# Two of the four rows of attention weights in each half of a head, turned by 32x32 blocks and DMAs through DRAM

## The chip, the cores and the metric

The kernel runs on one core of one Trainium2 chip. The metric is device time in microseconds (us) of one execution: 1113.87 us before the change, the median of three runs (1113.86 to 1114.06). The engines are named as in the profile: PE is TensorE (matmuls and transposes; PEld its weight loads), DVE is VectorE, ACT is ScalarE, POOL is GpSimd, and SP is the engine whose queue issues every DMA of this kernel. SBUF is the memory of 128 partitions beside the engines, PSUM the one that PE writes, DRAM the large one outside.

## What is computed

A trunk of two layers over 1024 positions of width 1024 in float32: a gated linear recurrence (RG-LRU), then an attention layer with a forget gate (FoX), each with a norm ahead and a residual, and a final norm. The change concerns the attention:

```python
def fox_mixer(h, w_in, b_f, w_out):          # 16 heads of 64
    q, k, v, gate, f_logit = ...              # slices of h @ w_in
    cum = cumsum(log_sigmoid(f_logit + b_f))
    def one_block(q_blk, cq_blk, start):      # 128 queries
        logits = einsum("bqhd,bkhd->bhqk", q_blk, k) / 8
        logits = logits + (cq_blk[..., :, None] - ck[:, :, None, :])
        logits = where(kpos <= qpos, logits, -1e30)
        p = softmax(logits)
        return einsum("bhqk,bkhd->bqhd", p, v)
    ...
    return (o * silu(gate)) @ w_out
```

## The kernel before

Almost every product is a sum of three: both factors are split into a high part that TensorE's float32r takes exactly and a low part (the rest), and high times high, high times low and low times high are added in PSUM. So each operand costs a rounding copy (to_hi, mostly ACT, L87) and a subtraction (to_lo, mostly DVE or POOL, L98). In the attention products the weights p are split and V comes with both parts side by side.

The recurrence layer fills the span up to about 405 us; its last projection, keys, queries, gates, values and the sums of the forget gate take it to about 510 us. From there to about 1086 us the 16 heads run one after the other, and the span ends with the last projection, the norm and the stores (tile "turn", L57 and L918 to L976).

A head has two halves c of 512 queries, and a half four rows i of 128 queries (i = 4c to 4c+3). Row i sees (i+1) blocks of 128 keys.

- maxima(hd, c) is a generator with one step a row: PE makes the logits S[queries, keys] (L57, tile S), DVE adds the mask and takes the row maximum (L731), ACT takes the exponential with its sum (L736) into p{i}, [128 queries, (i+1) x 128 keys]. Rows go in ascending order. A last step inverts the sums and sends them through DRAM (recd, recb), from where POOL scales the gate (L765).
- weigh(hd, c) needs p with the keys on the partitions. In steps of two key blocks it transposes every 128x128 block of p on PE against an identity (L61, tile pt in PSUM), ACT rounds the result into ph, DVE subtracts into pl, and PE adds V x ph and V x pl into O (L57). The products of a step are held until the step after it (held). A last step adds the halves of O (L810, L811).
- fill is a generator of other matmuls that don't depend on this head: keys, queries and gates of the next pair of heads, or for the last four heads the output projection. One unit is six matmuls of 512 columns.

The order on PE is written out by hand. In each of the strings below a digit is a step of that generator and a dot is a unit of fill; in the first, 0 is weigh(hd, 0) and 1 is maxima(hd, 1), in the second 0 is weigh(hd, 1) and 1 is maxima(hd + 1, 0). What is left of a generator is run at the end. Heads 12 to 15 have LAST, with more fill.

```python
ORDER = "1.0.1.1.1.0.0", "10.1.0.1.01.0.0"
LAST = "1..0.1..1..1.0.0", "10..1.0.1.01..0..0"
```

Each step on PE is put behind the one before with issue_after. The other engines' instructions are ordered by the scheduler of the tile framework and run in that order; where a tile is used again, the new writer waits for the old readers. S and pt share one tag of two PSUM buffers, ph and pl have three SBUF tiles each, and each p{i} has one.

All DMAs are issued by SP, in order. Weight tiles come through the tag "wf", four tiles (L108, L360, L533, L984), are split, and are used by PE. At the end of head hd, load(hd + 2) (L621 to L635) brings keys and queries of the head after the next into T and U, as soon as PE no longer reads them.

## Time and profile before

| | |
|---|---|
| timed, median of 3 | 1113.87 us |
| profiled execution, its own time | 1113.94 us |
| its span (first to last instruction) | 1112.2 us |
| granted clock of TensorE | 1.00 |
| DMA | 105.43 MB in 63558 packets, 31.1% of 16 engines' span |
| transposes of p on PE (L61) | 576 |
| splits of pt into ph and pl | 198 on ACT, 198 on DVE |

How to read the rows that follow in the prediction. A group has line, engine, operation, tiles "out<-in", shape and count, then busy us and mean ns of one, then the idle time of the engine just ahead of them and what ended it. A row of the timeline has start, length, engine, line, operation, tiles and count. A wait has who waited for whom, us in total, times and the longest. In a window stand its ends and length, then busy us (and instructions) of PE, PEld, DVE, ACT and POOL, the granted clock, the share of the DMA engines and GB/s. Matmuls overlap, so the mean of one is longer than the distance from one to the next.

### The profile page before, as it was taken

What the parts mean: (1) busy time and instruction counts of PE and PEld (TensorE: products, weight loads), DVE (VectorE), ACT (ScalarE), POOL (GpSimd) and SP (SyncE); (2) the same over time, 40 slices, a digit from 0 to 9 for tenths busy, and PEclk for the clock granted to TensorE, in tenths of its full rate; (3) what the DMA queues carried; (4) which work ended last, traced back from release to release, by engine and by line L of the source; (5) the groups of instructions that cost most, each with busy time, mean ns of one, the idle gap of its engine ahead of it and who ended that gap; (6) DMA issues with size and microseconds to landing.
All of it is one profiled execution on the core that took longest, in us unless ns stands there. A gap on an engine that the chain in (4) does not pass through costs nothing.

```text
span 1112.2 us, 15778 instructions
## 1 busy us (share of the span) xinstructions
PE 1101.9 (99%) x5697; PEld 935.1 (84%) x5697; DVE 755.0 (68%) x1266; ACT 582.4 (52%) x1075; POOL 166.1 (15%) x120
## 2 busy tenths in 40 slices
PE   9999999999999999999999999999999999999997
PEld 7787888888888888988888988889888898878886
DVE  8888755876669687756676566765667655576645
ACT  8487445355453665544555355544555544454435
POOL 1222212111111201421110100101002020010110
PEclk9999999999999999999999999999999999999999
DMA  6111111111112113443334224242142431655444
GB/s 239 48 57 43 51 54 43 48 53 42 62 35 75 48 54 129 129 112 118 101 90 103 91 69 109 72 113 96 53 122 75 103 108 38 185 159 185 142 147 189
DMA packets 63558, 105.43 MB, mean 95 GB/s; under 512 B 9364, under 2 KB 24340, under 8 KB 63480
## 3 DMA queue, kind: packets, MB, share of 16 engines
q1 hardware_dynamic: 63480, 104.42, 31.1%
q8 instruction: 45, 0.74, 0.3%
q14 instruction: 33, 0.27, 0.1%
HBM read 63.30 MB, written 15.93 MB: 71 GB/s over the span
## 4 chain that ended last, share of the span: by engine, by line
PE 93%; issue 3%; DVE 1%; ACT 1%; POOL 1%; DMA 1%; SPq 0%; DVEq 0%; POOLq 0%; ACTq 0%
PE gps L57 33%; PE ops L57 17%; PE ups L57 10%; PE vps L57 8%; PE S L57 6%; PE O L57 6%; PE pt L61 6%; PE turn L57 3%; PE gate L57 2%; POOL wl L98 1%; PE sscol L57 0%; DMA x<-in_xt 0%; DVE hl L232 0%; PE rsrow L57 0%; DMA wf<-in_w 0%
## 5 line engine op out<-in xcount | busy, mean ns | idle before, releaser
L57 PE MATMUL gps<-hh,wh 128*128 128x512 f32 x576 | 228.2, 396 | 0.0
L57 PE MATMUL gps<-hh,wl 128*128 128x512 f32 x576 | 225.6, 392 | 0.2 <-POOL wl L98 0.2
L57 PE MATMUL gps<-hl,wh 128*128 128x512 f32 x576 | 225.5, 392 | 0.0
L87 ACT CAST wh<-wf 128x512 fp32r<-128x512 f32 (+2 forms) x156 | 94.0, 607 | 141.8 <-PE gps L57 56.0
L736 ACT ACTIVATE p<-S,m 128x128 f32<-128x128 f32 (+7 forms) x128 | 94.9, 741 | 140.0 <-DVE m L731 139.1
L98 POOL TENSOR_TENSOR wl<-wf,wh 128x512 fp32r<-128x512 f32 (+1 forms) x60 | 95.6, 1600 | 382.2 <-ACT wh L87 321.7
L98 DVE TENSOR_TENSOR pl<-pt,ph 128x512 fp32r<-128x512 f32 (+1 forms) x198 | 98.7, 540 | 77.0 <-ACT ph L87 76.3
L57 PEld LDWEIGHTS gps<-hl,wh 128*128 128x128 f32 x576 | 108.2, 188 | 23.8
L57 PEld LDWEIGHTS gps<-hh,wl 128*128 128x128 f32 x576 | 108.5, 188 | 19.2 <-POOL wl L98 0.6
L57 PEld LDWEIGHTS gps<-hh,wh 128*128 128x128 f32 x576 | 108.5, 188 | 19.0
L731 DVE CUSTOM_DVE_ANT_0 S<-S,mask 128x128 f32<-128x128 f32 (+7 forms) x128 | 97.3, 760 | 34.2 <-PE S L57 29.6
L765 POOL TENSOR_TENSOR sg<-sg,recb 64x512 f32<-64x512 f32 x32 | 42.8, 1356 | 441.9 <-DMA recb<-recd 407.3
L87 ACT CAST ph<-pt 128x512 fp32r<-128x512 f32 (+1 forms) x198 | 83.5, 472 | 29.1 <-PE pt L61 23.9
L57 PE MATMUL S<-T,U 96*128 96x512 f32 (+7 forms) x384 | 91.7, 347 | 0.0
L98 DVE TENSOR_TENSOR wl<-wf,wh 128x512 fp32r<-128x512 f32 x96 | 68.3, 719 | 24.6 <-ACT wh L87 23.8
L375 DVE TENSOR_TENSOR x<-x,ops 128x512 f32<-128x512 f32 x80 | 54.1, 681 | 40.3 <-PE ops L57 40.3
L57 PEld LDWEIGHTS S<-T,U 128*128 128x128 f32 (+1 forms) x384 | 68.7, 189 | 12.5 <-ACT p L736 0.2
L61 PE MATMUL pt<-ident,p 128*128 128x128 f32 x576 | 79.2, 273 | 0.0
L61 PEld LDWEIGHTS pt<-ident,p 128*128 128x128 f32 x576 | 67.5, 140 | 11.5 <-issue 2.1
L57 PE MATMUL ups<-hh,wh 128*128 128x512 f32 x192 | 75.4, 394 | 1.0 <-ACT hh L89 0.4
L57 PE MATMUL ups<-hh,wl 128*128 128x512 f32 x192 | 75.0, 391 | 0.6 <-POOL wl L98 0.6
L57 PE MATMUL ups<-hl,wh 128*128 128x512 f32 x192 | 75.2, 391 | 0.2 <-DVE hl L232 0.2
(163 smaller groups left out, 2245.4 us busy)
## 6 DMA issues: line engine op xcount, KB each, us to landing
wf<-in_w SPq DMA_DIRECT2D x100, 256.0 KB
wf<-in_wo SPq DMA_DIRECT2D x64, 128.0 KB
U<-qkh SPq DMA_DIRECT2D x64, 128.0 KB
T<-qkh SPq DMA_DIRECT2D x28, 256.0 KB
x1d<-x SPq DMA_DIRECT2D x16, 256.0 KB
wf<-in_wv SPq DMA_DIRECT2D x16, 256.0 KB
U<-qkl SPq DMA_DIRECT2D x32, 128.0 KB
xp<-x1d SPq DMA_DIRECT2D x16, 256.0 KB
```

What stands on the lines that cost most here:

```text
L57: pe[0] = nc.tensor.matmul(*args, **kw)
L61: pe[0] = nc.tensor.transpose(*args)
L87: nc.scalar.copy(hi, src)
L98: return eng.tensor_tensor(lo, src, f32(hi), ALU.subtract)
L375: nc.vector.tensor_tensor(x, x, pt, ALU.add)
L731: masked[0] = nc.vector.tensor_tensor_reduce(S[:, :n], S[:, :n], mask[:, SEQ - n :], -1.0, -NEG, ALU.add, ALU.min, accum_out=m)
L736: seen[0] = nc.scalar.activation(p, S[:, :n], AF.Exp, bias=m, scale=-1.0, accum_out=sums[:, i : i + 1])
L765: nc.gpsimd.tensor_tensor(sg, sg, recs[hd // 2][rows, part], ALU.mult)
```

## The change

In every half but the lower half of head 0 (by_dma), the two longest rows of the four, i % 4 = 2 and 3, are turned without PE, except for the diagonal block of the longest (key block 4c+3), which PE still transposes.

- The two rows of a half lie in one tile (tag pp0 or pp1, two_rows): 2 x (4c+3) key blocks and the diagonal block behind them. This takes the place of p2, p3 and p6, p7.
- After the exponential of such a row, turn_row has DVE transpose its 4c+3 key blocks by 32x32 blocks into a tile "turn" (one buffer, 128 x 384 or 128 x 896), with an order of the columns in which each of the four quarters m of a key block is contiguous. A DMA on SP stores it into DRAM (turnd). After the second of the two rows, four more DMAs read it back, one for each m, into 32 partitions of the same tile from which the rows came, in runs of (4c+3) x 128 bytes.
- The rows go in descending order (reversed), in every half.
- weigh has near pieces, transposed by PE into PSUM as before, and far pieces, [128, 8, 32] views of the tile of two rows in SBUF (far_rows). Both are split into one ph and one pl, the near pieces first; the products are as they were. Where all rows of a key block are far, it has no near piece.
- To make room, wf has three tiles in place of four, fz, cp and res take other tags.

```diff
-        a = wpool.tile([P, room], F32, tag="wf", name="wf", bufs=4)[:, :n]
+        a = wpool.tile([P, room], F32, tag="wf", name="wf", bufs=3)[:, :n]
...
-        fz = const.tile([P, 8, HEADS], F32, name="fz")
+        fz = at.tile([P, 8, HEADS], F32, tag="yo", name="fz", bufs=2)
...
+        two_rows = {}
+        turnd = [dram.tile([P, 2, (4 * c + 3) * P], F32, name=f"turnd{c}") for c in range(2)]
+
+        def row_tile(i, n):
+            c, r = i // 4, i % 4 - 2
+            if r < 0:
+                return at.tile([P, n], F32, tag=f"p{i}", name="p", bufs=1)
+            size = (4 * c + 3) * P
+            if r:
+                two_rows[c] = at.tile([P, 2 * size + P], F32, tag=f"pp{c}", name="pp", bufs=1)
+            return two_rows[c][:, r * size : r * size + n]
+
+        def by_dma(hd, c):
+            return hd > 0 or c == 1
+
+        def turn_row(i, p):
+            c, r = i // 4, i % 4 - 2
+            nk = 4 * c + 3
+            t = at.tile([P, 7 * P], F32, tag="turn", name="turn", bufs=1)[:, : nk * P]
+            nc.vector.transpose(
+                t.rearrange("p (m k q) -> p k m q", m=4, q=32),
+                p[:, : nk * P].rearrange("p (k m q) -> p k m q", m=4, q=32),
+            )
+            nc.sync.dma_start(turnd[c][:, r], t)
+            if r == 0:
+                to = two_rows[c][:, : 2 * nk * P].rearrange("p (r b f) -> p r b f", r=2, b=4)
+                src = turnd[c].rearrange("(b p) r (m f) -> m p r b f", b=4, m=4)
+                for m in range(4):
+                    nc.sync.dma_start(to[32 * m : 32 * m + 32], src[m])
+
+        def far_rows(c):
+            return two_rows[c][:, : (8 * c + 6) * P].rearrange("p (b k q) -> p b k q", b=8, q=32)
...
-            for i in range(4 * c, 4 * c + 4):
+            for i in reversed(range(4 * c, 4 * c + 4)):
...
-                p = ps_[i] = at.tile([P, n], F32, tag=f"p{i}", name="p", bufs=1)
+                p = ps_[i] = row_tile(i, n)
...
+                if i % 4 > 1 and by_dma(hd, c):
+                    turn_row(i, p)
...
-                for jj in range(2):
-                    ks = slice((j0 + jj) * P, (j0 + jj + 1) * P)
-                    for q in range(qlo[jj], end, P):
-                        o = q - qlo[jj]
-                        transpose(A[:, jj, o : o + P], ps_[q // P][:, ks], ident)
...
+                near, far = [], []
+                for jj, j in enumerate((j0, j0 + 1)):
+                    rows = range(qlo[jj] // P, end // P)
+                    away = [i for i in rows if i % 4 > 1 and j < 4 * c + 3] if by_dma(hd, c) else []
+                    own = [i for i in rows if i not in away]
+                    for o, i in enumerate(own):
+                        transpose(A[:, jj, o * P : (o + 1) * P], ps_[i][:, j * P : (j + 1) * P], ident)
+                    w = len(own) * P
+                    near.append((A[:, jj, :w], slice(0, w)))
+                    far.append((j, slice(4 * (away[0] % 4) - 8, 8), slice(w, ns[jj])) if away else None)
...
+                for lo in range(2):
+                    for (ph, pl), (src, to) in zip(parts, near):
+                        if to.stop:
+                            split(src, ph[:, to], pl[:, to], lo)
+                for lo in range(2):
+                    for (ph, pl), f in zip(parts, far):
+                        if f:
+                            j, b, to = f
+                            split(far_rows(c)[:, b, j], *(z[:, to].rearrange("p (b q) -> p b q", q=32) for z in (ph, pl)), lo)
```

Here split(src, hi, low, lo) is to_hi on ACT for lo = 0 and to_lo on DVE for lo = 1.

More of the change, by code (lines that the diff above doesn't have):

```diff
@@ L267, in split_gates @@
         def split_gates(n):
-            wt = wpool.tile([P, 4, P], F32, tag="wf", name="wgf", bufs=4)[:, :2]
+            wt = wpool.tile([P, 4, P], F32, tag="wf", name="wgf", bufs=3)[:, :2]
             nc.sync.dma_start(wt, wg[n])
@@ L356, in out_weights @@
         def out_weights(g, d0, parts=wpool):
-            wt = wpool.tile([P, 4, P], F32, tag="wf", name="wf", bufs=4)
+            wt = wpool.tile([P, 4, P], F32, tag="wf", name="wf", bufs=3)
             for j in range(2):
@@ L531, in value_weights @@
                 if k < KT:
-                    wt = wpool.tile([P, 2, 256], F32, tag="wf", name="wf", bufs=4)
+                    wt = wpool.tile([P, 2, 256], F32, tag="wf", name="wf", bufs=3)
                     nc.sync.dma_start(wt, wv[g, :, k : k + 2])
@@ L658, in forget @@
             e_ = at.tile([HEADS, HALF], F32, tag="ph", name="e", bufs=3)
-            parts = [at.tile([HEADS, HALF], F32R, tag=f"p{i + 2 * half}", name="cp", bufs=1) for i in (3, 4)]
+            parts = [at.tile([HEADS, HALF], F32R, tag=t, name="cp", bufs=1) for t in (("p4", "p5"), ("pp1", "turn"))[half]]
             hi, lo = parts
@@ L782, in products, with split @@
                     matmul(o, v, pl, start=False, stop=j == nj - 1)
+            def split(src, hi, low, lo):
+                if lo:
+                    to_lo(low, src, hi, nc.vector)
+                else:
+                    to_hi(hi, src, nc.scalar)
             held = None
@@ L788, in weigh @@
                 ns = [end - q for q in qlo]
[L789 to L801 removed]
+                near, far = [], []
[8 more added lines that the diff above has]
+                    far.append((j, slice(4 * (away[0] % 4) - 8, 8), slice(w, ns[jj])) if away else None)
+                parts = [
+                    tuple(at.tile([P, HALF], F32R, tag=t, name=t, bufs=3)[:, :n] for t in ("ph", "pl")) for n in ns
+                ]
+                for lo in range(2):
[7 more added lines that the diff above has]
+                            split(far_rows(c)[:, b, j], *(z[:, to].rearrange("p (b q) -> p b q", q=32) for z in (ph, pl)), lo)
                 if held:
@@ L931, in turned @@
             else:
-                res = [tu.tile([P, SEQ], F32, tag="U1", name="res"), at.tile([P, SEQ], F32, tag="p7", name="res", bufs=1)]
+                res = [tu.tile([P, SEQ], F32, tag="U1", name="res"), at.tile([P, SEQ], F32, tag="pp1", name="res", bufs=1)]
             for b in range(2):
@@ L981, in late @@
                 for b in range(2):
-                    wt = wpool.tile([P, 4, P], F32, tag="wf", name="wf", bufs=4)
+                    wt = wpool.tile([P, 4, P], F32, tag="wf", name="wf", bufs=3)
                     for d in range(2):
```

8 lines of the change are left out of this document (removed).

## The prediction

> **What bounds the kernel now.** The page comes first: the busy times, then the chain that ended last.
>
> ```profile
> span 1112.2 us, 15778 instructions
> PE 1101.9 (99%) x5697; PEld 935.1 (84%) x5697; DVE 755.0 (68%) x1266; ACT 582.4 (52%) x1075; POOL 166.1 (15%) x120
> PE 93%; issue 3%; DVE 1%; ACT 1%; POOL 1%; DMA 1%; SPq 0%; DVEq 0%; POOLq 0%; ACTq 0%
> by line: PE gps L57 33.2%; PE ops L57 17.1%; PE ups L57 10.0%; PE vps L57 8.4%; PE S L57 6.4%; PE O L57 6.2%; PE pt L61 5.7%; issue 3.4%; PE turn L57 2.6%; PE gate L57 2.3%; POOL wl L98 0.7%; PE sscol L57 0.4%; DMA x<-in_xt 0.4%; DVE hl L23
> ```
>
> TensorE (PE) is busy in 1101.9 of 1112.2 us, and 93% of the chain is PE, one matmul behind the other. Time taken from PE's queue is therefore time taken from the kernel, as long as no new wait opens on PE. The last row, the same chain by line from the view of the chain, has "PE pt L61 5.7%", which is what the change cuts: the transposes of attention weights. The list of waits by engine shows how much PE waits for the engines that feed it:
>
> ```profile
> PEld O L57 <- DVE pl L98: 0.3, 1, 0.3
> DVE pl L98 <- ACT ph L87: 76.3, 70, 3.4
> ACT wh L87 <- DMA wf<-in_wo: 7.4, 3, 3.7
> ```
>
> Over the whole kernel the weighted sums waited once, 0.3 us, for a low part that DVE makes. The 76.3 us that DVE waited for ACT were covered. The stages differ, so here are windows: 616:757 is one period of four heads, 930:1086 the last four.
>
> ```profile
> 616.00:757.00 141.00, 141.00 (x823) 123.26 (x821) 89.33 (x189) 71.53 (x164) 16.41 (x12) 1.00 0.33 91
> 930.00:1086.00 156.00, 154.80 (x804) 129.90 (x802) 98.67 (x201) 72.65 (x169) 15.57 (x12) 1.00 0.48 150
> ```
>
> Columns: length, busy time of PE, PEld, DVE, ACT, POOL, granted clock, DMA share, GB/s. PE is full in the first and nearly so in the second; DVE has 89.3 of 141 us, ACT 71.5, the DMA engines a third.
>
> The profiled execution took 1113.94 us, 1.74 beyond its span; the three timed runs have a median of 1113.87. I count from 1113.94.
>
> **Removed from PE.** A head's lower half has 1+2+3+4 = 10 transposes, its upper half 5+6+7+8 = 26. Of the two longest rows of each half all but the diagonal block of the last row leave PE: 3+3 = 6 below, 7+7 = 14 above. Head 0 keeps its lower half: 15 x 6 + 16 x 14 = 314 of 576. What one costs:
>
> ```profile
> L61 PE MATMUL pt<-ident,p 128*128 128x128 f32 x576 | 79.2, 273 | 0.0
> 546.06 1.04 PE L61 MATMUL pt<-ident,p 128*128 128x128 f32 x8
> ```
>
> The mean of 273 ns overlaps its neighbours; 79.2/576 = 0.138 us is an upper end. 5.7% of 1112.2 us gives 0.110 each; eight in 1.04 us, less the last one's tail of about 0.16, give the same. I take 0.110: **314 x 0.110 = 34.5 us**, 2.2 per full head. The products (L57) keep their number and widths, since near and far parts land in one ph and one pl.
>
> **Added to DVE and ACT.** 32 block transposes of 128x896 and 30 of 128x384. The trace has none. Nearest rows of those widths, one source with one pass on DVE:
>
> ```profile
> L731 DVE CUSTOM_DVE_ANT_0 S<-S,mask 128x896 f32<-128x896 f32 x16 | 17.6, 1099 | 14.8 <-PE S L57 14.7
> L731 DVE CUSTOM_DVE_ANT_0 S<-S,mask 128x384 f32<-128x384 f32 x16 | 8.9, 557 | 1.6 <-PE S L57 1.6
> L342 DVE TENSOR_TENSOR_SCAN a<-a,ti 128x1024 f32<-128x1024 f32 x11 | 30.1, 2738 | 0.2
> 1095.19 2.74 DVE L1075 TENSOR_SCALAR res<-res,ssq 128x1024 f32<-128x1024 f32 x4
> ```
>
> I take 1.10 and 0.56 us: 32 x 1.10 + 30 x 0.56 = 52 us. The slow end is the scan, 2.67 ns a column: 2.4 and 1.0 us, 108 us in all; the fast end is the scaling of 1024 columns in 2.74/4 = 0.69 us: 0.61 and 0.26, 27 us. [...]
>
> Splitting into near and far makes more pieces. Heads 1 to 14 have 2+2+1+1 = 6 in place of 4, and 14 in place of 8; head 0 has 14 for 8 above, head 15 two more below: 198 become 318.
>
> ```profile
> L87 ACT CAST ph<-pt 128x512 fp32r<-128x512 f32 x91 | 50.9, 588 | 19.6 <-PE pt L61 19.1
> L87 ACT CAST ph<-pt 128x256 fp32r<-128x256 f32 x43 | 15.3, 368 | 9.5 <-PE pt L61 4.8 <-issue 2.9 <-ACT sq L951 1.7
> L98 DVE TENSOR_TENSOR pl<-pt,ph 128x512 fp32r<-128x512 f32 x91 | 60.0, 687 | 59.0 <-ACT ph L87 58.6
> L98 DVE TENSOR_TENSOR pl<-pt,ph 128x256 fp32r<-128x256 f32 x43 | 17.8, 423 | 18.1 <-ACT ph L87 17.7
> ```
>
> Halving the width takes 588 to 368 ns and 687 to 423, so the fixed part is 0.15 us on ACT and 0.16 on DVE: 120 more pieces are 18 and 19 us. Together DVE gets some 4.5 us a full head: 89.3 + 18 = 107 us in a period that shrinks from 141 to 132, four fifths busy. It still has room, but no longer much in the stretches with long rows; there a transpose stands behind a mask pass or a pl and delays those behind it.
>
> **Added to the queues.** 31 half heads x 6 DMAs = 186, all on SP: two stores (0.46 MB each above, 0.20 below) and four loads into 32 partitions each, in runs of 896 or 384 bytes. That is 41 MB on top of 105. The loads wait for both stores, and SP issues in order: weight loads, T and U loads and the sums' round trip stand behind. The first cover is the spare tile that a weight load has; its ACT waits above (7.4 us, three times) never reached PE.
>
> **The step that decides** is the way back of the upper half. In the head below, S rows go out in four slots; 536.10 is the second, 546.06 the first transposes of weigh(1,1), 550.74 the first product that needs them.
>
> ```profile
> 531.89 0.81 PE L57 MATMUL S<-T,U 128*128 128x320 f32 x4
> 536.10 0.87 PE L57 MATMUL S<-T,U 128*128 128x512 f32 x4
> ...
> 549.95 1.03 PE L61 MATMUL pt<-ident,p 128*128 128x128 f32 x8
> 550.74 0.48 PE L57 MATMUL O<-ph,v 128*128 128x512 f32 x1
> ```
>
> From 536.10 to 550.74 are 14.64 us. With the order turned round, rows 6, 5, 4 and the next head's 3 and 2 stand there in place of 5, 6, 7, 0 and 1: 3200 columns either way. Ten transposes less (2+4+4) make it 14.64 - 1.10 = **13.5 us of room** between row 6's S and the first product. What has to fit in, first for row 6 as it is now:
>
> ```profile
> 538.20 0.97 PE L57 MATMUL S<-T,U 128*128 128x512 f32 x4
> 539.21 1.10 DVE L731 CUSTOM_DVE_ANT_0 S<-S,mask 128x896 f32<-128x896 f32 x1 [0.62 <-PE S L57]
> 540.40 1.01 ACT L736 ACTIVATE p<-S,m 128x896 f32<-128x896 f32 x1 [1.33 <-DVE m L731]
> 541.31 0.19 ACT L736 ACTIVATION_READ_ACCUMULATOR p<-S,m 128x1 f32 x1
> ```
>
> 538.20 to 541.50 are 3.3 us to the end of the exponential. The transpose adds 1.1. For the store and the loads:
>
> ```profile
> 1039.69 0.32 SPq L902 DMA_DIRECT2D x1d<-xp  x1
> 1041.69 0.32 SPq L898 DMA_DIRECT2D xp<-x1d  x1
> SPq L898 <- DMA x1d<-xp: 19.6, 12, 3.1
> 543.00:546.00 3.00, 3.00 (x19) 2.62 (x18) 2.35 (x7) 1.63 (x5) 0.00 (x0) 1.00 1.01 210
> 1097.00:1101.00 4.00, 4.00 (x24) 3.35 (x23) 3.35 (x8) 2.08 (x5) 0.00 (x0) 1.00 1.02 419
> ```
>
> A store of 256 KB into DRAM was over 2.0 us after its issue (the next load into that buffer waits for it). Full-width DMAs moved 419 GB/s, T and U loads into 64 partitions 210, both with the DMA engines full. The store of 0.46 MB is then 2.0 + 0.2 MB/419 = 2.5 us. The four loads move 0.92 MB: 4.4 us at 210, 2.2 at 419, and 2.0 - 0.6 = 1.4 fixed. I take 210, as the transfers are narrow: 5.8 us. First far pieces: ACT 0.4, DVE 0.4. Sum: 3.3 + 1.1 + 2.5 + 5.8 + 0.8 = **13.5 us, no slack at all**; with 419 it is 11.3, and 2.2 spare. [...]
>
> So each queue on the way becomes a wait on PE. Known ones: "turn" is single, and row 6's transpose (due 4.1 + 3.3 = 7.4 us after the first slot; the slots lie 531.89 to 536.10 apart) needs row 7's store landed (3.7 + 1.1 + 2.5 = 7.3), a tie. DVE has mask, pl and weight splits beside it: half a us to one. Most of all, odd heads load T and U for two heads later as soon as the fourth row is done:
>
> ```profile
> 541.29 0.46 SPq L621 DMA_DIRECT2D T<-qkh  x1
> ...
> 543.12 1.12 SPq L632 DMA_DIRECT2D U<-qkh  x1
> 544.29 1.23 SPq L633 DMA_DIRECT2D U<-qkh  x1
> 545.61 0.55 SPq L634 DMA_DIRECT2D U<-qkl  x1
> ```
>
> That is 5.2 us after the second slot, just when row 6's store is under way (4.4 to 6.9). Three T loads, 0.77 MB, are queued before the loads of the rows, some 3.7 us at 210 GB/s, of which about two fall on our loads; issues of over 1.1 us show the queue full. My estimate of the wait on PE: 1 us in an even head, 2.6 in an odd one, 1.8 as a mean, in heads 0 to 11: 22 us. [...]
>
> ```profile
> 479.07 2.77 PE gps L57 x12
> 548.32 0.40 PE L57 MATMUL S<-T,U 128*128 128x256 f32 x2
> 572.36 0.48 PE L57 MATMUL O<-ph,v 128*128 128x512 f32 x1
> ```
>
> A unit of fill is six matmuls, 1.4 us by the first row (a piece of the chain: start, us, what). Heads 12 to 15 have three units more in that stretch, which I take to cover it. The lower half has time: its row 2 goes out in the slot at 548.32, its first product comes at 572.36, 24 us on, against about 9.
>
> Costed at nothing: wf from four tiles to three (a weight load has about three tiles of PE time, 5.5 us each, for a landing of some 2 to 3; if that cover goes, a few us in the first stage); the moved fz, cp and res tiles; the reversed rows in head 0.
>
> Sum: 1113.9 - 34.5 + 22 = **1101 us**.
>
> **Rivals.**
> *All hidden*: the loads run at full width, or DVE and SP place them well; wait under 0.9 us a head, 1079 to 1090. For it: 2.2 us spare by the 419 row. Against: the 210 row and the T loads.
> *The way back is too long (slower)*: place, the first products of weigh(hd,1) in heads 0 to 11. Each us beyond the room costs 12 us; from 34.5/12 = 2.9 us a head the change loses. With 4 us it is 1113.9 - 34.5 + 48 = 1127. For it: no slack in the sum, one SP queue, ACT blocked behind a far copy that hasn't landed. Against: PE stalls also give DVE and DMA time.
> *DVE bound*: by the scan's rate DVE gets 6.8 + 1.2 us a head, 89.3 + 32 = 121 of 132 us, in order and with waits for ACT between; I put the wait on PE at what it gains or a little more, 1114 to 1125. Against: the mask rows, half that price, are one pass too.
> *Not as said*: if PE transposes shrink less than 314 the count shows it; I give that nothing.
>
> **How the numbers follow.** Forecast (wait 0.9 to 2.7 us, 1090 to 1111) 0.41; all hidden 0.22; near the break-even 0.08; way back too long 0.24; DVE bound 0.05. 0.2% of 1114 is 2.2 us, about what a measurement of this kernel can tell from no change: faster 0.63, same 0.08, slower 0.29. The range takes most of the hidden and of the slower cases: 1081 to 1131.
>
> **What would show it.** x262 transposes (L61) at 0.11 us. PE below 99% in 505:930, with a wait "O <- DVE pl" or behind "ph <- DMA" once a head, longer in odd heads; nothing new before 500 us. DVE near 80% there, transposes at 1.1 us. If PE stays full, the way back was hidden; if DVE is full, its price was wrong; if waits stand at S or gps in place of O, a queue I took as covered (ACT, weights) is the bound.

## The result and the profile after

The changed kernel takes 1176.05 us (median of four runs, 1170.71 to 1180.44) against 1113.88 for the kernel before: a ratio of 1.0556, 95% interval 1.051 to 1.0601. It is slower by 62 us, where 1101 was forecast and 1131 was the upper end of the range.

From the page of the changed kernel, its span, PE's busy time and the chain by engine:

```profile
span 1178.7 us, 15829 instructions
...
PE 1106.6 (94%) x5383; PEld 914.7 (78%) x5383; DVE 810.0 (69%) x1448; ACT 597.9 (51%) x1195; POOL 171.8 (15%) x120
...
PE 70%; DMA 9%; DVE 8%; ACT 5%; issue 4%; SPq 3%; POOL 0%; ACTq 0%; DVEq 0%; POOLq 0%
```

TensorE has 314 transposes less and yet as much busy time as before (1101.9; matmuls at a granted clock of 0.50 behind some waits, and the 0.16 us by which a row ahead of a wait outlasts the next possible start, both below, fill it up), and it stands idle in 1178.7 - 1106.6 = 72.1 us, where it stood in 10.3. The chain that ended last has turned from 93% PE into 70%; the rest is DMA, DVE, ACT and SP. The view of windows (ends, length, busy us of PE, PEld, DVE, ACT and POOL, granted clock, DMA share, GB/s), one row for the first heads, one for each period of four heads, one for the last four:

```profile
505.00:641.53 136.53, 120.64 (x569) 96.12 (x567) 95.17 (x216) 67.65 (x175) 14.97 (x11) 0.95 0.59 165
641.53:802.47 160.94, 146.10 (x741) 120.26 (x741) 104.83 (x236) 75.64 (x197) 15.93 (x12) 0.94 0.52 144
802.47:964.22 161.75, 143.60 (x764) 119.61 (x765) 105.69 (x241) 77.54 (x202) 16.71 (x13) 0.97 0.53 147
964.22:1154.59 190.37, 175.77 (x903) 146.74 (x904) 120.58 (x259) 83.23 (x214) 16.37 (x13) 0.97 0.59 179
```

A period of 141.0 us with a full PE has become one of 161 with 15 to 18 us idle. DVE is not full: 105 of 161 us. Nothing was lost ahead of the heads: PE transposes the sums of head 0 at 515.95 us, where it did at 515.76. The clock, 1.00 before, is 0.94 to 0.97.

From the groups of instructions by shape:

```profile
L98 DVE TENSOR_TENSOR pl<-pp,ph 128x256 fp32r<-128x256 f32 x157 | 72.8, 483 | 51.4 <-ACT ph L87 38.2 <-DMA U<-qkh 9.5 <-PE tr L784 2.8
...
L87 ACT CAST ph<-pp 128x256 fp32r<-128x256 f32 x157 | 60.0, 410 | 61.6 <-DMA pp<-turnd 43.0 <-DMA U<-qkh 9.6 <-PE O L57 5.8
...
L98 DVE TENSOR_TENSOR pl<-pt,ph 128x256 fp32r<-128x256 f32 x96 | 36.9, 411 | 11.5 <-ACT ph L87 11.2
...
L729 DVE STREAM_TRANSPOSE turn<-pp 128x896 f32<-128x896 f32 x32 | 35.5, 1111 | 15.8 <-ACT pp L771 13.9 <-DMA turnd<-turn 1.5 <-issue 0.2
L61 PE MATMUL pt<-ident,p 128*128 128x128 f32 x224 | 35.3, 273 | 3.4 <-DVE pl L98 3.4
...
L87 ACT CAST ph<-pt 128x256 fp32r<-128x256 f32 x96 | 33.0, 372 | 43.4 <-PE pt L61 40.3 <-issue 3.0
...
L729 DVE STREAM_TRANSPOSE turn<-pp 128x384 f32<-128x384 f32 x30 | 17.1, 569 | 10.2 <-DMA turnd<-turn 6.5 <-ACT ph L87 3.7
...
L61 PE MATMUL pt<-ident,pp 128*128 128x128 f32 x38 | 9.9, 279 | 0.0
```

The transposes left on PE are 224 + 38 = 262. The new work came at its price on DVE, 1.11 and 0.57 us, and with 157 far pieces. A far piece of 256 columns takes 410 ns on ACT and 483 on DVE, one from PSUM 372 and 411. The list of waits (who waited for whom, us in total, times, longest) shows where the loss stands:

```profile
ACT ph L87 <- DMA pp<-turnd: 43.0, 14, 4.9
...
PEld O L57 <- ACT ph L87: 37.6, 12, 5.5
```

ACT waits 14 times for the rows that come back from DRAM, and behind it PE waits 12 times, once in each of heads 0 to 11, for the first upper product (37.6 us by the weight loads, PEld; 34.8 by the matmuls themselves). Four of these, heads 4 to 7, on PE's timeline, with the idle time and what ended it in brackets:

```profile
680.91 0.49 PE L57 MATMUL O<-ph,v 128*128 128x512 f32 x1 [0.80 <-ACT ph L87]
...
720.04 0.80 PE L57 MATMUL O<-ph,v 128*128 128x512 f32 x1 [4.92 <-ACT ph L87]
...
752.81 0.50 PE L57 MATMUL O<-ph,v 128*128 128x512 f32 x1 [1.63 <-ACT ph L87]
...
786.93 0.50 PE L57 MATMUL O<-ph,v 128*128 128x512 f32 x1 [3.16 <-ACT ph L87]
```

Short in even heads, long in odd ones. SP's timeline says why, first for the even head that ends with the wait at 680.91, then for the odd one with that at 720.04 (start, length, line, tiles):

```profile
671.32 0.32 SPq L733 DMA_DIRECT2D turnd<-turn  x1
...
673.86 2.58 SPq L738 DMA_DIRECT2D pp<-turnd  x4
...
706.54 0.64 SPq L622 DMA_DIRECT2D T<-qkh  x1
707.27 0.54 SPq L733 DMA_DIRECT2D turnd<-turn  x1
707.86 1.14 SPq L623 DMA_DIRECT2D T<-qkl  x1
709.09 1.55 SPq L632 DMA_DIRECT2D U<-qkh  x1
...
712.41 0.61 SPq L738 DMA_DIRECT2D pp<-turnd  x1
```

In the even head the store of row 6 (671.32) has landed after 2.5 us and the four loads follow at 673.86; ACT can read them at 680.45, 6.6 us later (6.6 to 7.5 in the six even heads):

```profile
680.45 0.40 ACT L87 CAST ph<-pp 128x256 fp32r<-128x256 f32 x1 [2.85 <-DMA pp<-turnd]
```

In the odd head the store lies between loads of T and U, and 5.1 us go by before the loads of the rows start; SP issues without a pause in between. Whether that is the order of the queue or the bytes is one question for the runs.

### The profile page after: what moved, and what is told of

Same layout as the page of the kernel before. It is cut to its first block, busy times and chain, and to the rows that moved or that the text cites. A ratio compares the mean times of both kernels' runs of the same rounds, so it can differ in the third digit from the quotient of the medians.

```text
span 1178.7 us, 15829 instructions
## 1 busy us (share of the span) xinstructions
PE 1106.6 (94%) x5383; PEld 914.7 (78%) x5383; DVE 810.0 (69%) x1448; ACT 597.9 (51%) x1195; POOL 171.8 (15%) x120
## 4 chain that ended last, share of the span: by engine, by line
PE 70%; DMA 9%; DVE 8%; ACT 5%; issue 4%; SPq 3%; POOL 0%; ACTq 0%; DVEq 0%; POOLq 0%
PE gps L57 23%; PE ops L57 15%; PE ups L57 9%; PE vps L57 7%; PE S L57 5%; DMA pp<-turnd 4%; PE O L57 4%; DMA turnd<-turn 3%; PE turn L57 2%; DVE pl L98 2%; PE gate L57 2%; SPq L738 2%; PE pt L61 1%; ACT ph L87 1%; DVE S L766 1%
## 5 line engine op out<-in xcount | busy, mean ns | idle before, releaser
L57 PE MATMUL gps<-hh,wh 128*128 128x512 f32 x576 | 232.8, 404 | 0.0
L57 PE MATMUL gps<-hh,wl 128*128 128x512 f32 x576 | 229.8, 399 | 0.1
L98 POOL TENSOR_TENSOR wl<-wf,wh 128x512 fp32r<-128x512 f32 (+1 forms) x60 | 102.1, 1706 | 375.8 <-ACT wh L87 262.1
L766 DVE CUSTOM_DVE_ANT_0 S<-S,mask 128x512 f32<-128x512 f32 (+7 forms) x128 | 96.8, 756 | 22.7 <-PE S L57 22.5
L57 PE MATMUL S<-T,U 128*128 128x512 f32 (+7 forms) x384 | 96.6, 360 | 13.1 <-ACT p L771 6.7
L98 DVE TENSOR_TENSOR pl<-pp,ph 128x256 fp32r<-128x256 f32 x157 | 72.8, 483 | 51.4 <-ACT ph L87 38.2
L57 PE MATMUL O<-ph,v 128*128 128x512 f32 (+1 forms) x198 | 73.7, 379 | 34.8 <-ACT ph L87 34.8
L87 ACT CAST ph<-pp 128x256 fp32r<-128x256 f32 x157 | 60.0, 410 | 61.6 <-DMA pp<-turnd 43.0
L771 ACT ACTIVATE pp<-S,m 128x512 f32<-128x512 f32 (+1 forms) x64 | 54.6, 853 | 62.8 <-DVE m L766 62.7
L87 ACT CAST ph<-pt 128x256 fp32r<-128x256 f32 (+2 forms) x161 | 48.5, 333 | 60.6 <-PE pt L61 57.2
```

Source lines behind the costliest of these rows:

```text
L57: pe[0] = nc.tensor.matmul(*args, **kw)
L87: nc.scalar.copy(hi, src)
L98: return eng.tensor_tensor(lo, src, f32(hi), ALU.subtract)
L766: masked[0] = nc.vector.tensor_tensor_reduce(S[:, :n], S[:, :n], mask[:, SEQ - n :], -1.0, -NEG, ALU.add, ALU.min, accum_out=m)
L771: seen[0] = nc.scalar.activation(p, S[:, :n], AF.Exp, bias=m, scale=-1.0, accum_out=sums[:, i : i + 1])
```

## The experiments

Each run is compared with the kernel before on the same chip, 1113.9 to 1114.6 us each time. Where a run leaves part of the computation out, its expectation says which.

### What the way back costs, by halves and by itself

Without the six DMAs of a half head (e1), only the upper half by DMA (e2), only the lower (e3), and the kernel before with its rows reversed (e4), in this order:

```diff
-            nc.sync.dma_start(turnd[c][:, r], t)
-            if r == 0:
...
-                for m in range(4):
-                    nc.sync.dma_start(to[32 * m : 32 * m + 32], src[m])
```

```diff
-            return hd > 0 or c == 1
+            return c == 1
```

```diff
-            return hd > 0 or c == 1
+            return hd > 0 and c == 0
```

```diff
-            for i in range(4 * c, 4 * c + 4):
+            for i in reversed(range(4 * c, 4 * c + 4)):
```

> Leaves out the six DMAs of each half: VectorE still turns the rows by blocks, and the far pieces are split straight from the rows as they are, so the sums are of unturned blocks. Theory A (the way back through DRAM decides, PE waits for it and then runs at a lower granted clock): with the trip gone PE is full again, 1079 to 1086 us, granted clock 1.00. Theory B (SP's one queue and the single turn tile hold everything up): the same, this run doesn't tell it from A. Theory C (the added work of VectorE and ScalarE is the bound): 1120 us or more, with PE waiting for pl or S. Theory D (fewer weight tiles, or the reversed rows): 1120 or more too.

> Far rows only in the upper halves (224 transposes off PE, 96 of 186 DMAs). A: nearly all of the loss is here; lower halves gave back at most their 9.9 us, so 1170 to 1185. B: the loss is shared over both halves' DMAs, some 1135 to 1150. C: by VectorE's time (two thirds of it here) 1140 to 1155. D: 1176 as before.

> Far rows only in the lower halves of heads 1 to 15 (90 transposes off PE, 90 DMAs). A: these rows have over 20 us until their products, so the 9.9 us come out nearly whole: 1104 to 1109. B: 1125 to 1140, with VectorE's transpose waiting for the turn tile and SP's queue behind the loads. C: 1115 to 1125. D: 1150 or more.

> The kernel before, with the rows of a half in descending order and nothing else. A, B and C: within 3 us of 1114, PE full. D: the order is at least part of the loss, 1125 or more.

| run | us | ratio | interval |
|---|---|---|---|
| no round trip | 1110.87 | 0.9969 | 0.9957 to 0.9982 |
| upper half only | 1160.96 | 1.0416 | 1.04 to 1.0431 |
| lower half only | 1138.93 | 1.022 | 1.0191 to 1.025 |
| order only | 1127.24 | 1.0117 | 1.0102 to 1.0132 |

None of the four theories of the first run had its time, and none that of the second. The round trip is worth 1176.05 - 1110.87 = 65 us. But without it the change still gains only 3 of the 34.5 us that its transposes took on PE. Some 31 us go elsewhere. The lower half, which I had taken for covered, loses 25 us by itself, as theory B had it (DVE's transposes wait 12 times there, 15.4 us in all, for the one turn tile), and the reversed order 13. From the waits of the run with the lower half alone:

```profile
PEld pt L61 <- DVE pl L98: 15.2, 19, 2.4
```

In the kernel before this wait came once, with 0.2 us; here transposes stand 19 times behind the low parts of an earlier pt whose PSUM buffer they need.

### Order, lower half

The run without the round trip, rows ascending again (e9), and the lower half alone with ascending rows, a turn tile for each of its two rows (in the two xp buffers) and four wf tiles (e5). Both have the first change, e5 the others too (in both the tile of two rows is now made by the first row and the loads follow the second; those lines are left out):

```diff
-            for i in reversed(range(4 * c, 4 * c + 4)):
+            for i in range(4 * c, 4 * c + 4):
```

```diff
-            return hd > 0 or c == 1
+            return hd > 0 and c == 0
...
-            t = at.tile([P, 7 * P], F32, tag="turn", name="turn", bufs=1)[:, : nk * P]
+            t = at.tile([P, 7 * P if c else HALF], F32, tag=("xp", "turn")[c], name="turn", bufs=2 - c)[:, : nk * P]
...
-        a = wpool.tile([P, room], F32, tag="wf", name="wf", bufs=3)[:, :n]
+        a = wpool.tile([P, room], F32, tag="wf", name="wf", bufs=4)[:, :n]
```

> The run without the round trip (the far pieces read unturned rows: left out), but the rows in the old ascending order. Theory A (the order costs 13 us by itself, and it adds to the rest): 1110.9 - 13.4, 1095 to 1100 us; what is left over 1079.4 (1113.9 less 34.5) is the added DVE and ACT work. Theory B (the added DVE and ACT work is the loss and the order costs nothing beside it): 1108 to 1113 us. Theory C (order is the whole loss): 1079 to 1086 us.

> Only the lower half by DMA, rows in the old ascending order, a turn tile for each of its two rows, four wf tiles as before. Theory A (the lower half lost 25 us in the run with the lower half alone because of the reversed order, 13 us, and because its second turn waits for the one turn tile and its store stands behind others on SP): both are gone, row 3 still has about 15 us to the first product of the next head's lower half against a chain of about 10, so 90 transposes less, 9.9 us, minus 2 to 5 us for more work on DVE and ACT: 1104 to 1110 us, four-head period 139 to 140.5. Theory B (the chain of the lower half is itself too long, or the ACT queue stands at the far pieces): over 1118 us, with ACT ph <- DMA pp<-turnd above 10 us and PE waiting behind it.

e9 took 1111.43 us, the same as with reversed rows: theory B. So the 13 us of the order don't add to the rest: with ascending rows too the added work takes what PE had been spared, and PE then waits at O for low parts (12.3 us, 16 times). e5 took **1108.95 us** (0.9955, 0.994 to 0.997), as theory A said: it is the one version that leaves nothing out and beats the kernel before, by 5 us or half a per cent. Its page:

```profile
PE 1093.0 (99%) x5607; PEld 925.5 (84%) x5607; DVE 770.0 (70%) x1326; ACT 584.6 (53%) x1105; POOL 166.5 (15%) x120
```

PE is full again. From head 4 to head 8 (the transposes of the sums, at 655.22 and 793.71) a period takes 138.5 us in place of 141.0, and 24 transposes less account for that at 0.105 us each. So the price of a transpose was right, and where the way back has time the whole gain comes home, from those heads at least (over all heads 5 of 9.9 us). The lower half alone lost 30 us more with the order, the tile and the buffer that the change gave it; which of the three counts most was not separated.

### Where the 31 us go that the round trip doesn't take

The run without the round trip, without the DVE transposes too (e11), then with four wf tiles besides (e15, the second change turned round); and the kernel before with three (e17, the second change):

```diff
-                if i % 4 > 1 and by_dma(hd, c):
-                    turn_row(i, p)
```

```diff
-        a = wpool.tile([P, room], F32, tag="wf", name="wf", bufs=4)[:, :n]
+        a = wpool.tile([P, room], F32, tag="wf", name="wf", bufs=3)[:, :n]
```

> The run without the round trip, and without VectorE's block transposes as well (left out: round trip and 32x32 transposes; the far pieces read the weights as they are). Against 1110.9 with the transposes and 1079.4 if nothing but TensorE's 34.5 us had changed. Theory A (the 52 us of transposes on DVE are what PE then waits for): 1084 to 1096 us. Theory B (the far pieces of ph and pl, a second short instruction on ACT and on DVE for each, are): 1104 to 1111 us.

> The run without turn and round trip (1108.3; the same is left out here), with four wf tiles as before. Theory A (the fourth buffer was cover: with three, TensorE waits 3.6 and 1.3 us for weight casts in heads 14 and 15 and about 1 us before the first head): 1101 to 1104 us, and those waits gone. Theory B (three are as good as four, the casts are late because ACT has more to do): 1106 to 1110 us.

> The kernel before with three wf tiles and nothing else changed. Theory A (the fourth buffer was cover in the kernel before too): 1117 to 1122 us. Theory B (it covers nothing unless SP or ACT are held up by the change): 1113.5 to 1115 us.

Measured were 1108.26 us (0.9946, 0.9929 to 0.9964), 1104.74 (0.9907, 0.9892 to 0.9922) and 1115.20 (1.0004, 0.9994 to 1.0013). So the 52 us of transposes on DVE cost 2.6 us, the fourth wf buffer 3.5 (nothing in the kernel before, where nothing else was late; both theories of e15 hold half), and what is left is 1104.7 - 1079.4 = 25 us for the second, short instruction of each split together with the order and the tile that two rows share; no run takes these apart, but their place shows in the trace. From ACT's and then PE's timeline of e15:

```profile
658.55 0.65 ACT L87 CAST ph<-pt 128x256 fp32r<-128x256 f32 x2 [0.25 <-PE pt L61]
659.09 0.72 ACT L87 CAST ph<-pp 128x256 fp32r<-128x256 f32 x2
659.70 0.70 ACT L765 ACTIVATE pp<-S,m 128x512 f32<-128x512 f32 x1
```

```profile
659.51 0.40 PE L57 MATMUL gps<-hl,wh 128*128 128x512 f32 x1
660.54 0.62 PE L57 MATMUL S<-T,U 128*128 128x384 f32 x2 [0.64 <-ACT pp L765]
```

Two near casts, two far ones, and only then the exponential of row 3, which empties the PSUM buffer that row 2's S needs. PE started a matmul at 659.51 and could have started the next 0.23 us later; it started at 660.54, 0.80 late, of which the profile marks 0.64 as idle, since the row of the last matmul lasts 0.40 us, up to 659.91. Eight waits of 0.17 to 0.65 us in a period make 3.6 us marked as idle, and with 0.16 each, by which a row of 0.39 outlasts the 0.23 us to the next possible start, 4.9 us. That is most of what a period lost: 80 transposes less should have brought it from 141.0 to 132.2 us, and it took 137.8. The third buffer shows in e11, ACT and PE in head 14, where a cast waits for its weight and the projection for the cast:

```profile
1024.87 0.62 ACT L87 CAST wh<-wf 128x512 fp32r<-128x512 f32 x1 [1.87 <-DMA wf<-in_wo]
```

```profile
1025.55 0.50 PE L57 MATMUL ops<-yhh,wh 128*128 128x512 f32 x1 [3.56 <-ACT wh L87]
```

### What makes the way back late

Lower turns in the two xp buffers (e6), one unit of fill more ahead of the first upper product (e7), no T and U loads (e8), and the same loads issued by POOL (e10, every DMA of load and load_q), in this order:

```diff
-            t = at.tile([P, 7 * P], F32, tag="turn", name="turn", bufs=1)[:, : nk * P]
+            t = at.tile([P, 7 * P if c else HALF], F32, tag=("xp", "turn")[c], name="turn", bufs=2 - c)[:, : nk * P]
```

```diff
-ORDER = "1.0.1.1.1.0.0", "10.1.0.1.01.0.0"
+ORDER = "1.0.1.1.1.0.0", "10.1..0.1.010.0"
```

```diff
-            if hd + 2 < HEADS:
+            if hd + 2 < 0:
                 load(hd + 2, us=(0,) if hd % 2 == 0 and hd < 12 else (0, 1))
```

```diff
-            nc.sync.dma_start(f32(T[s][:64, 0, cs]), hi)
+            nc.gpsimd.dma_start(f32(T[s][:64, 0, cs]), hi)
```

> The changed kernel with the lower half's two turn tiles in the xp buffers (two of 512 columns), so that the turn of row 2 waits for no store. Theory A (the single tile, costed as a tie, is a wait of its own): the 8.0 us of waits at the turn go, and with them the late pl pieces, pt and S behind them and part of the clock lost there: 1160 to 1168 us. Theory B (the tile is only where the SP queue's order shows; the store of row 3 still goes out late behind recb and row 2's far pieces then wait for the loads): 1172 to 1180 us, the wait moving to the far pieces of the lower half.

> The changed kernel with one fill unit (1.36 us of TensorE work) moved from ahead of the last two steps of the second run to ahead of the step that holds the first upper product of heads 0 to 11. Theory A (the round trip is simply longer than the room that the order leaves): each of the 12 waits at the first upper product falls by about 1.4 us or to nothing, their sum from 35 us to 18 to 21, and with less idle time some clock comes back: 1150 to 1160 us. Theory B (the transfers are late for another reason, or the moved unit is missed where it was): 1168 to 1182 us.

> The changed kernel without the loads of T and U for heads 2 to 15 (left out: these heads use the scores of stale T and U tiles; the late half of U is still loaded). Theory A (in odd heads the store of row 6 lands behind the T and U loads): the six waits at the first upper product in odd heads fall from 4.4 us to the 1.4 of even heads, 18 us, and some of the lost clock comes back: 1148 to 1158 us. Theory B (odd heads are longer for another reason, as their fill units): odd waits stay above 3.5 us, 1168 to 1178 us.

> The changed kernel with the loads of T and U issued by POOL and not by SP; the same bytes. Theory A (what the run without these loads gained, 29 us, was the order of SP's queue): the odd heads' waits fall to those of even heads here too: 1146 to 1156 us. Theory B (it was the bytes, which share the DMA engines with the way back): 1165 to 1178 us. If POOL's own work (sg, yo, wl) is held up by the issues, waits for POOL appear on PE or DVE.

| run | us | ratio | interval |
|---|---|---|---|
| two turn tiles | 1170.99 | 1.0517 | 1.0496 to 1.0538 |
| more room | 1172.94 | 1.0529 | 1.0513 to 1.0544 |
| no T and U loads | 1146.98 | 1.0291 | 1.0273 to 1.0308 |
| T and U loads by POOL | 1191.19 | 1.0696 | 1.0674 to 1.0717 |

The first two can't be told from the changed kernel (interval 1.051 to 1.0601). Both missed the time of theory A. In e6 the waits for the turn tile went (8.0 us to 0.7); in e7 the waits at the first upper product fell nearly as theory A had it, from 34.8 us to the first of these rows:

```profile
PE O L57 <- ACT ph L87: 21.7, 10, 4.1
PE S L57 <- DVE pl L98: 6.8, 6, 2.8
...
PE pt L61 <- DVE pl L98: 6.2, 9, 1.3
PE S L57 <- ACT pp L771: 5.3, 7, 1.5
```

But the unit was missed where it had been: the last three rows were 4.8, 3.4 and 1.1 us in the changed kernel. The room moved, the time didn't. The T and U loads are worth 29 us, a little more than theory A of e8 had. The first upper product in heads 4 and 5, without these loads and with them on POOL's queue:

```profile
669.25 0.49 PE L57 MATMUL O<-ph,v 128*128 128x512 f32 x1 [0.74 <-ACT ph L87]
...
703.00 0.80 PE L57 MATMUL O<-ph,v 128*128 128x512 f32 x1 [2.60 <-ACT ph L87]
```

```profile
684.29 0.50 PE L57 MATMUL O<-ph,v 128*128 128x512 f32 x1 [0.48 <-ACT ph L87]
...
722.45 0.80 PE L57 MATMUL O<-ph,v 128*128 128x512 f32 x1 [6.88 <-ACT ph L87]
```

0.80 and 4.92 us became 0.74 and 2.60 without the loads, but 0.48 and 6.88 when another queue issued them. The mean of the 12 waits in e8 is 1.4 us; in the odd heads of e10 they are 5.6 to 7.0. SP's timeline of e10, in the odd head, shows the store and the loads of the rows behind the second of these waits:

```profile
706.86 0.32 SPq L733 DMA_DIRECT2D turnd<-turn  x1
...
710.37 4.80 SPq L738 DMA_DIRECT2D pp<-turnd  x4
```

The way back has two legs, from the store of row 6 to the loads of the rows, and from there to the first product. In the changed kernel the odd heads lose on the first: 4.1 to 5.6 us against 2.5 in even heads, with the T and U loads issued in between. The second leg takes 7.5 to 8.3 us in odd heads, hardly more than the 7.1 to 7.9 in even ones. In e10 the first leg of the odd heads is shorter, 2.9 to 3.8 us, but the second grows to 11.3 to 12.2. So SP's order is part of what the odd heads of the changed kernel wait for, some 1.5 us of it, and yet another queue doesn't help: there the T and U loads run beside the loads of the rows, which then take 4 us longer. Whether their bytes do that or the way POOL issues them (POOL is busy for 271.8 us in e10, for 171.8 in the changed kernel) was not separated. e10 was worse than either theory allowed.

### The lower clock

Behind some of the waits matmuls come at half their rate, and the view of windows gives the granted clock with it: 0.50 from 689.90 to 695.40 us, 1.00 from 667 to 680. Two rows of the changed kernel ahead of a wait, then the wait at 689.32 and what follows:

```profile
667.69 0.39 PE L57 MATMUL gps<-hh,wl 128*128 128x512 f32 x1
667.91 0.39 PE L57 MATMUL gps<-hl,wh 128*128 128x512 f32 x1
...
689.32 0.79 PE L57 MATMUL S<-T,U 128*128 128x256 f32 x2 [1.43 <-ACT p L771]
689.91 0.63 PE L57 MATMUL gps<-hh,wh 128*128 128x512 f32 x1
690.33 0.63 PE L57 MATMUL gps<-hh,wl 128*128 128x512 f32 x1
```

Starts are 0.22 us apart ahead of it and 0.42 behind it, up to 695.4. Added up over the timeline's rows of 512 columns from 480 us on, such stretches make some 38 us, so about 19 us of matmul work were lost in them. To see what that is worth, e12 puts 12 matmuls (2.7 us) into the waits of odd heads:

```diff
                     with tc.issue_after(pe[0].ins):
+                        if c == 1 and j0 == 2 and hd % 2 and hd < 12:
+                            for _ in range(12):
+                                matmul(O, V[0][:, 2 * s : 2 * s + 2].rearrange("p a d -> p (a d)"), hT[0][0][0], start=True, stop=True)
                         products(*held)
```

> The changed kernel with 12 matmuls of 512 columns more (2.7 us of TensorE at full clock, into the O buffer that the first product then starts afresh) ahead of the first upper product of the odd heads 1 to 11, where TensorE waited 3.2 to 5.3 us. Theory A (idle TensorE time is what halves its rate behind these waits): the half-rate stretches behind the six waits, 21.6 us long, go or shrink, at no cost since the added work lies inside the waits: 1162 to 1168 us, clock 0.983 to 0.988. Theory B (the rate falls for another reason): 1174 to 1182 us, clock still 0.974 to 0.978.

The clock rose to 0.988, from 0.976, and the stretches shrank to some 23 us, as theory A said; yet the time was 1177.8 us (1.0572, 1.0556 to 1.0588), as theory B said, and can't be told from the changed kernel. From head 0 to head 12 the profiled execution was 6.6 us shorter (475.8 for 482.3 us), and the rest of its span 3.8 us longer; runs of the changed kernel alone lie 10 us apart, so these two are a pointer and no more. In PE's waits a new row shows part of what ate it:

```profile
PE vps L57 <- ACT wh L87: 6.7, 3, 3.0
```

Three times PE now stands ahead of the values, waiting for weights. With work in the waits less time goes at half rate (23 us for 38), but winning part of the rate back gave no time that shows: what PE gained in heads 0 to 11 seems to have been waited for behind them. Why the last four heads, where nothing was edited, took longer stays open.

### Pieces that are needed late

If the way back only needs time, it should pay for the pieces that are used last: six in each half, key blocks 0 to 2 below and 4 to 6 above, rows ascending, 186 transposes less (e14). e16 does so in heads 0 to 11 alone and moves the lower half's first far casts one step later (with one step more for it in the order strings); e18 fixes their place behind the last row's exponential.

```diff
-                    away = [i for i in rows if i % 4 > 1 and j < 4 * c + 3] if by_dma(hd, c) else []
+                    away = [i for i in rows if i % 4 > 1 and 4 * c <= j < 4 * c + 3] if by_dma(hd, c) else []
```

```diff
-            return hd > 0 or c == 1
+            return hd < 12 and (hd > 0 or c == 1)
...
+                if j0 == 0 and c == 0:
+                    yield
                 for lo in range(2):
                     for (ph, pl), f in zip(parts, far):
```

```diff
+                            if j0 == 0 and c == 0 and lo == 0:
+                                ctx_ = tc.issue_after(seen[0].ins)
+                            else:
+                                ctx_ = ExitStack()
+                            with ctx_:
```

The first is e14's main line (its smaller tiles are left out), the second is added by e16, the third by e18, for the casts of the step at j0 = 0 in the lower half.

> Ascending rows; in each half the last two query blocks of the last three full key columns only (6 pieces of a head and half, key blocks 0 to 2 in the lower, 4 to 6 in the upper half) by DVE and DMA, the rest by TensorE; turn tiles in the xp buffers. In the upper half these pieces are used two steps later than the first ones, some 15 us behind row 7. Theory A (the way by DMA pays where its deadline is later than its chain of about 10 us): 186 transposes less, 20.5 us, of which the lower half alone kept 5.2 of 9.9: 1098 to 1104 us. Theory B (the added pieces on ACT and DVE are waited for in the upper half as they were without the round trip): 1106 to 1114 us.

> The late pieces of both halves in heads 0 to 11 only, and the lower half's far pieces of the first two key blocks split one step later (behind the last row's exp), so that ACT does not stand at them ahead of the next rows' exps; three wf tiles. Theory A (standing ACT and the last heads were the loss): 143 transposes less, 15.7 us, less about 5 for pieces and 3 to 4 for the third wf buffer: 1101 to 1108 us. Theory B (the pieces themselves, each two more short instructions on the way to a product, cost more than the transposes): 1112 to 1122 us.

> As the run with the deferred late pieces, with the lower half's far casts of the first two key blocks now fixed on ACT behind the exponential of the upper half's last row. Theory A (ACT standing ahead of exponentials is what those heads lose): the waits S <- ACT p of 2.3 us in heads 2, 6 and 10 go, and these heads fall from 32 to 35 us to 29 to 30: 1108 to 1116 us. Theory B (ACT's place is not it; the loads are late and something waits for them anyway, the first lower product in place of S): 1119 to 1128 us.

In this order they took 1129.15 (1.0141, 1.0123 to 1.0158), 1126.45 (1.0095, 1.0075 to 1.0115) and 1142.28 us (1.026, 1.0233 to 1.0288): my theory A missed three times; e14 and e18 came out above theory B too, and e16 at 1126.45 above its 1122. ACT and PE of e14:

```profile
713.85 0.71 ACT L87 CAST ph<-pp 128x256 fp32r<-128x256 f32 x2 [4.82 <-DMA pp<-turnd]
714.47 0.89 ACT L775 ACTIVATE p<-S,m 128x768 f32<-128x768 f32 x1
```

```profile
715.51 0.50 PE L57 MATMUL S<-T,U 128*128 128x512 f32 x1 [1.53 <-ACT p L775]
```

ACT stands 4.82 us at the lower half's far piece, the exponential of row 5 stands behind it, and the next S waits for that. e16 didn't change this: the scheduler left the casts where they were in ACT's order (there the wait is 5.68 us). In e18 they did move, and the heads that had been long, 2, 6 and 10, fell from 35.1, 33.4 and 32.1 us in e16 to 29.5, 31.2 and 28.9, nearly as A said. In exchange nearly every head now waits at the first lower product:

```profile
PE O L57 <- ACT ph L87: 16.7, 11, 1.5
```

and the gates' tanh, whose buffer a turn now uses, waits for the store. That e5 gains with the lower half and e14 doesn't with both isn't settled further; the second half doubles the DMAs, and SP, ACT and the xp buffers are all shared.

## Why the prediction was wrong

One change at a time, from the sum without any wait to the changed kernel. The runs come from several chips, on which the kernel before took 1113.9 to 1114.6 us, so a step is uncertain by a us or two; of the two small ones, that of wf is clear of it, that of the transposes on DVE barely:

| | us | step |
|---|---|---|
| 1113.9 - 34.5, transposes gone and nothing added | 1079.4 | |
| near and far pieces, rows reversed (e15) | 1104.7 | +25.3 |
| three wf tiles (e11) | 1108.3 | +3.5 |
| transposes on DVE (e1) | 1110.9 | +2.6 |
| stores and loads of the rows (e8) | 1147.0 | +36.1 |
| T and U loads beside them (after) | 1176.1 | +29.1 |

By the prediction's own steps:

- **Removed from PE**: right. 262 transposes are left, and e5 gives 0.105 us for one where nothing waits, against 0.110.
- **Added to DVE and ACT**: the count (318) and the DVE transposes (1.11 and 0.57 us, against 1.10 and 0.56) were right; that the transposes would hide was right but for 2.6 us. That the 120 more pieces would hide was the **first step that failed**. I judged DVE by its busy share, four fifths, and found room. The pieces lie in a chain: transposes, casts, low parts, and the buffer that the next S needs. On that chain every short instruction counts, full engine or not, and it cost 25 us (the order adds nothing to that: e9 and e1 take the same time). That it is the pieces is argued, not shown: the round trip, the DVE transposes, the third wf tile and the order are left out one by one, and PE then waits where the pieces stand; no run leaves out the pieces alone. Their price was low as well: near plus far is 782 ns against 588 on ACT and 894 against 687 on DVE, 0.19 and 0.21 us more rather than 0.15 and 0.16.
- **The step that decides**: place, alternation of heads and the store (2.5 us) were right, the loads took 6.6 to 7.5 us in even heads rather than 5.8. The **second step that failed** is the size of the wait and what I let it cost. Waits were 1.4 us in even heads and 4.4 in odd ones, 2.9 as a mean, against 1.0, 2.6 and 1.8. In the odd ones the T and U loads were given the right place, ahead of the loads of the rows, and too small a price: they put off the loads of the rows by 1.6 to 3.1 us, and the odd heads wait 3.0 us longer than the even ones, where the sum had 1.6. That SP's queue was full there, I read from the issues of two U loads, 1.12 and 1.23 us; issued at 533.32 and 533.83 the same lines take 0.46 and 0.59, and no view shows how full a queue is. And 12 x 2.9 = 35 us is only half of the 65, the rest of which I put at nothing. Between the profiled executions of e1 and of the changed kernel (67 us) PE's idle time grows by 42.8 us: 34.8 at the first upper product, 7.6 at the last projection, at pt and at S. PE's busy time grows by 24.5 us, some 19 of them in the stretches at half rate behind the waits; e12 warns that filling the waits doesn't win them back. So of the 75 us between forecast and result some 31 are the first step with wf and the DVE transposes, 13 are waits at this product beyond the 22 us of the sum, and 30 are what came with the waits.
- **Heads 12 to 15**: their fill covers the first upper product, which doesn't wait there. But from the sums of head 12 to the last ones they take 131.7 us in place of 119.2, with 10 us of waits for weights and inputs of the last projection, which the sum had at nothing.
- **Lower half has time**: its products had, but the one turn tile, DVE and the PSUM buffer had not; alone it loses 25 us.
- **Costed at nothing**: wf, 3.5 us when the rest of the change is there; reversed rows, 13 us by themselves, nothing on top of the pieces.
- **The rival that came true** is "the way back is too long", with the right place. Its price, 12 us for each us of wait, came to break-even at 2.9 us; the kernel has that wait and loses 62 us, as the pieces had taken nearly all of the gain already and PE loses as much again beside these waits.
- **What would show it**: the 262 transposes and the waits at O held. DVE was to be near 80% and is at 65 (105 of 161 us), because the period grew.

## What to carry to other kernels

Work taken from a full engine is worth its time only if the engines that now do it are off the chain (e15 took 1104.7 us where the whole gain would have been 1079.4), and a busy share doesn't tell that (DVE's is 105 of 161 us in the changed kernel): follow one buffer from writer to next writer and count the instructions between, short ones above all. A wait found at one place should be priced with what queues behind the waiting instruction in its engine's order; where three engines are near balance, moving room or filling a gap may only move the wait, as e7, e12 and e18 show. The one version that paid (e5) moved little, the lower half alone, in the old order and with the fourth wf tile left in place; a late deadline by itself was not enough (e14).

## What the runs showed of the hardware

- TensorE's rate halved behind some idle spells of 1.4 to 5.3 us, for up to 6.1 us (0.42 us from one matmul of 512 columns to the next against 0.22, granted clock 0.50 against 1.00), but not behind all: a wait of 1.43 us brought it at 689.32 (after waits of 0.80 and 0.73 within the 9 us ahead), one of 1.63 us at 752.81 with no other in the 10 us ahead of it, and one of 2.23 us at 849.40 didn't (0.23 us between starts behind it, clock 1.00 up to 852.00). What decides it was not shown.
- A split of 256 columns takes longer for a far piece, read from SBUF in runs of 32 columns, than for a near one, read from PSUM: 410 against 372 ns on ACT, 483 against 411 on DVE. No run separates the runs of 32 columns from the place.
- Four loads into 32 partitions each, 0.92 MB in all, in runs of 896 bytes, could be read 6.6 to 7.5 us after the first was issued, in the six even heads, where the large T and U loads lay elsewhere. In the odd heads of e10, with T and U loads on another queue beside them, it was 10.9 to 11.7 us.
